# Gate and up of a SwiGLU layer as a 2x2 block product, one pair of k-tiles in eight by Strassen's seven products

## The chip, the core and the metric

The kernel runs on one core of a Trainium2 chip. It uses TensorE (matrix products into PSUM, eight banks of 128 x 512 floats), VectorE and ScalarE (elementwise work, casts, evictions from PSUM), SyncE as the queue that issues the loads of weights, and ScalarE's queue for a few other transfers. The metric is device time in microseconds, the median of the runs shown; lower is better.

## The reference, cut to what matters

A decoder block over 256 tokens with a width of 2048: normalised input, projections, attention and mLSTM heads, an output projection with a residual, then the SwiGLU layer that is changed here, a gated embedding at the end. All inputs are float32.

```
h2 = rms_norm(x, w_norm_ffn[i])
x = x + (jax.nn.silu(h2 @ w_ffn_gate[i]) * (h2 @ w_ffn_up[i])) @ w_ffn_down[i]
```

h2 is 256 x 2048, w_ffn_gate and w_ffn_up are 2048 x 5632, w_ffn_down is 5632 x 2048.

## The kernel before, in words

Every large product goes through `linear` (line 210). The contraction is cut into k-tiles of 128 rows; the output into chunks of 512 columns; the 256 tokens into two blocks of 128 (b = 0, 1), each with its own PSUM accumulator, acc0 and acc1. A product in float32 is made of three matmuls on a reduced type: activations and weights are each split into a high half (a cast to float32r) and a low half (what the cast left off), and high x high, high x low of the weights, and low of the activations x high are added up in PSUM (lines 255, 256, 257). The activations are the stationary operand, 512 columns of weights stream past.

Weights come in pieces of two k-tiles, 128 x 1024 floats: a load on SyncE's queue into `wr` (line 229), ScalarE's cast to `wh` (line 230), VectorE's subtraction to `wl` (line 231). The pool `wpool` has four buffers of each. A piece serves 12 matmuls.

Gate and up take 11 chunks (`for c in range(NG)`, line 643). For a chunk, all 16 k-tiles of the gate weights go through `linear`, then ScalarE's sigmoid (line 649) and a multiply-add by VectorE (line 650) evict the two accumulators to `gg`; then the same for the up weights with one multiply-add each (line 653). The product is then split for the next layer by background tasks (`after_up`, `split_by_blocks`, `transposed`): VectorE transposes it in blocks of 32 (line 187, tile `tq`), ScalarE's queue writes it to DRAM in four transfers (`swap`, line 191) and reads it back in another layout (`quad`, line 196), and ScalarE and VectorE make high and low halves (lines 129, 130). `tq` and `quad` have one buffer each; `held` keeps two tasks from using them at once. The activations of the layer itself come in four quarters through the same path from the residual (lines 628, 133, 135).

The code is written as a stream; a scheduler then sets the order on each engine by its own estimate of times, and every engine runs its queue strictly in that order. After the last chunk the input p is loaded into a `gg0` buffer (line 660), transposed on TensorE (line 165) and split, and w_down's product follows.

## Time and profile before

| | us |
|---|---|
| median of three runs (1228.24 to 1229.06) | 1228.42 |
| the profiled execution | 1229.32 |
| span of its instructions | 1227.6 |
| TensorE busy | 1215.7 |
| VectorE busy | 706.0 |
| ScalarE busy | 585.9 |

A page of the profile gives busy time by engine; `PE` is TensorE's matmul, `PEld` its weight load, `DVE` VectorE, `ACT` ScalarE, `SPq` and `ACTq` the queues that issue transfers. `L231` is line 231 of the kernel. A matmul's printed duration is longer than the distance to the next one, since matmuls overlap.

### The profile page before, as it was taken

How to read it: one execution, taken by the hardware profiler on the slowest of the kernel's cores; microseconds unless marked ns; L12 is line 12 of the kernel's file. 1: busy time of each engine (PE TensorE's matmuls, PEld its weight loads, DVE VectorE, ACT ScalarE, POOL GpSimd, SP SyncE). 2: the span in 40 equal slices, each digit the busy share in tenths (PEclk: the TensorE clock that was granted, in tenths of full speed). 3: DMA queues.
4: the chain of work that ended last, by engine and by line, in shares of the span. 5: the costliest groups of instructions: out<-in, count | busy, mean ns of one | idle time of the engine just before them, and what ended most of it. 6: DMA issues, size and time to landing. Idle time of an engine off the chain costs nothing.

```text
span 1227.6 us, 15262 instructions
## 1 busy us (share of the span) xinstructions
PE 1215.7 (99%) x5675; PEld 1017.9 (83%) x5675; DVE 706.0 (58%) x948; ACT 585.9 (48%) x822; POOL 4.5 (0%) x24
## 2 busy tenths in 40 slices
PE   9999999999999999999999999999999999999998
PEld 6799978878888888888888888888888888888888
DVE  5566755555656655555665564655545555555754
ACT  6645555645545534443443443444444444446542
POOL 1000000000000000000000000000000000000000
PEclk9999999999999999999999999999999999999999
DMA  7578754675677776766776677677666666665672
GB/s 262 175 238 246 219 153 124 186 240 160 208 229 251 238 222 200 231 207 213 227 226 205 217 231 211 205 229 223 208 218 200 220 198 220 204 212 169 220 248 88
DMA packets 158781, 257.30 MB, mean 210 GB/s; under 512 B 10002, under 2 KB 54900, under 8 KB 158708
## 3 DMA queue, kind: packets, MB, share of 16 engines
q1 hardware_dynamic: 127156, 229.06, 59.6%
q10 hardware_dynamic: 31552, 27.28, 7.4%
q8 instruction: 44, 0.72, 0.2%
q14 instruction: 29, 0.24, 0.1%
HBM read 241.10 MB, written 15.20 MB: 209 GB/s over the span
## 4 chain that ended last, share of the span: by engine, by line
PE 88%; DMA 4%; DVE 3%; ACT 2%; issue 1%; ACTq 0%; SPq 0%; DVEq 0%
PE acc L256 29%; PE acc L257 28%; PE acc L255 28%; DMA wr<-in_w_in_dram 3%; DVE wl L231 1%; DMA wpost<-in_w_ple_post_norm_dram 1%; ACT wh L230 1%; ACT sq L116 1%; DMA quad<-swap 0%; DMA swap<-tq 0%; DVE m L376 0%; PE sc L551 0%; ACT act_h L690 0%; PE tr L165 0%; PE tr L568 0%
## 5 line engine op out<-in xcount | busy, mean ns | idle before, releaser
L231 DVE TENSOR_TENSOR wl<-wr,wh 128x1024 fp32r<-128x1024 f32 (+2 forms) x445 | 520.1, 1181 | 399.6 <-ACT wh L230 398.7
L230 ACT CAST wh<-wr 128x1024 fp32r<-128x1024 f32 (+2 forms) x445 | 447.2, 1018 | 519.4 <-PE acc L257 383.0
L255 PE MATMUL acc<-wh,act_h 128*128 128x512 f32 (+2 forms) x1568 | 593.1, 379 | 3.2 <-ACT wh L230 1.9
L256 PE MATMUL acc<-wl,act_h 128*128 128x512 f32 (+2 forms) x1568 | 591.4, 377 | 1.6 <-DVE wl L231 1.5
L257 PE MATMUL acc<-wh,act_l 128*128 128x512 f32 (+2 forms) x1568 | 591.2, 377 | 0.0
L255 PEld LDWEIGHTS acc<-wh,act_h 128*128 128x128 f32 x1568 | 294.6, 188 | 55.3 <-ACT wh L230 2.2
L256 PEld LDWEIGHTS acc<-wl,act_h 128*128 128x128 f32 x1568 | 294.8, 188 | 53.5 <-DVE wl L231 3.4
L257 PEld LDWEIGHTS acc<-wh,act_l 128*128 128x128 f32 x1568 | 294.7, 188 | 51.9 <-DVE act_l L135 0.6
L255 PE MATMUL acc<-wh,gh 128*128 128x512 f32 x224 | 88.0, 393 | 0.0
L256 PE MATMUL acc<-wl,gh 128*128 128x512 f32 x224 | 87.9, 393 | 0.0
L257 PE MATMUL acc<-wh,gl 128*128 128x512 f32 x224 | 87.1, 389 | 0.0
L257 PEld LDWEIGHTS acc<-wh,gl 128*128 128x128 f32 x224 | 42.0, 188 | 9.5
L255 PEld LDWEIGHTS acc<-wh,gh 128*128 128x128 f32 x224 | 42.1, 188 | 9.4
L256 PEld LDWEIGHTS acc<-wl,gh 128*128 128x128 f32 x224 | 42.1, 188 | 8.6
L133 ACT ACTIVATE act_h<-quad,vec_b 128x256 fp32r<-128x256 f32 x32 | 13.7, 498 | 22.5 <-DMA quad<-swap 22.5
L135 DVE SCALAR_TENSOR_TENSOR act_l<-quad,vec_b,act_h 128x256 fp32r<-128x256 f32 x32 | 13.5, 483 | 16.1 <-ACT act_h L133 16.1
L649 ACT ACTIVATE gg<-acc,rstd_ffn 128x512 f32<-128x512 f32 x22 | 15.1, 689 | 10.8 <-PE acc L257 10.8
L650 DVE SCALAR_TENSOR_TENSOR gg<-acc,rstd_ffn,gg 128x512 f32<-128x512 f32 x22 | 15.8, 751 | 4.7 <-ACT gg L649 4.5
L130 DVE TENSOR_TENSOR gl<-quad,gh 128x512 fp32r<-128x512 f32 x14 | 9.1, 688 | 16.2 <-ACT gh L129 16.2
L129 ACT CAST gh<-quad 128x512 fp32r<-128x512 f32 x14 | 8.0, 618 | 20.6 <-DMA quad<-swap 20.6
L653 DVE SCALAR_TENSOR_TENSOR gg<-acc,rstd_ffn,gg 128x512 f32<-128x512 f32 x22 | 15.4, 743 | 0.0
L116 ACT ACTIVATE sq<-xres 128x512 bf16<-128x512 f32 x24 | 14.9, 623 | 0.0
(192 smaller groups left out, 392.1 us busy)
## 6 DMA issues: line engine op xcount, KB each, us to landing
wr<-in_w_ffn_gate_dram SPq DMA_DIRECT2D x88, 512.0 KB, 4.3
wr<-in_w_ffn_up_dram SPq DMA_DIRECT2D x88, 512.0 KB, 4.7
wr<-in_w_ffn_down_dram SPq DMA_DIRECT2D x88, 512.0 KB, 4.6
wr<-in_w_in_dram SPq DMA_DIRECT2D x63, 512.0 KB, 4.8
wr<-in_w_in_dram SPq DMA_DIRECT2D x48, 344.0 KB, 3.8
wr<-in_w_out_dram SPq DMA_DIRECT2D x32, 512.0 KB, 4.7
wr<-in_w_ple_gate_dram SPq DMA_DIRECT2D x32, 512.0 KB, 4.7
swap<-tq ACTq DMA_DIRECT2D x100, 128.0 KB, 4.4
```

The lines of the kernel that those rows point to most:

```text
L116: nc.scalar.activation(sq[:, 0:n], src, AF.Square, accum_out=dst)
L130: nc.vector.tensor_tensor(lo, src, hi.bitcast(F32), op=ALU.subtract)
L133: nc.scalar.activation(part(dst[0], k + j, 1), src[:, j:j + 1], AF.Copy, scale=scales[j])
L135: nc.vector.scalar_tensor_tensor(part(dst[1], k + j, 1), src[:, j:j + 1], scales[j], part(dst[0], k + j, 1).bitcast(F32), op0=ALU.mult, op ...
L230: nc.scalar.copy(wh, wr)
L231: nc.vector.tensor_tensor(wl, wr, wh.bitcast(F32), op=ALU.subtract)
L255: nc.tensor.matmul(po[b][:, 0:n], ah[:, kk, s], wh[:, j, :], start=count == 1, stop=False)
L256: nc.tensor.matmul(po[b][:, 0:n], ah[:, kk, s], wl[:, j, :], start=False, stop=False)
L257: nc.tensor.matmul(po[b][:, 0:n], al[:, kk, s], wh[:, j, :], start=False, stop=count == total)
L649: nc.scalar.activation(gg[b], pg[b], AF.Sigmoid, scale=r)
L650: nc.vector.scalar_tensor_tensor(gg[b], pg[b], r, gg[b], op0=ALU.mult, op1=ALU.mult)
L653: nc.vector.scalar_tensor_tensor(gg[b], pu[b], rstd2[:, b:b + 1], gg[b], op0=ALU.mult, op1=ALU.mult)
```

## The change

The gate and the up weights of a chunk are taken together. A pair of k-tiles p (rows of A: two k-tiles of the activations, each with two token blocks; rows of B: the same two k-tiles of gate and of up) is a 2x2 by 2x2 block product with four outputs: gate and up for b = 0 and b = 1. Seven of the eight pairs are "plain" units: eight products, 24 matmuls, accumulated in four banks P2, P3, P4, P8 (tags acc0, acc1, acc0, acc1). Pair 1 is a "seven" unit: seven products P1 to P7, 21 matmuls, of sums of the blocks. P2, P3 and P4 go into the plain units' banks; P1, P5, P6, P7 have banks of their own (tags tr and sc, which are the banks of transposes and scores elsewhere), so all eight banks hold accumulators.

The sums of activation blocks are made once (`make_forms`, in the first chunk); the sums of weight blocks (`t12`, `t34`) by VectorE for every chunk, and they are split into halves like weights. So a plain unit has two casts and two subtractions of 1024 columns; the seven unit has three and a half of each, four buffers. In the first chunk the seven unit stands fourth, in the others first. P1, P6, P7 and P5 are evicted into `qr` (tile quad) and `su` (tile tq) some units later, P2, P4, P3, P8 at the end of the chunk. `gg` has one buffer for each b now; `p_sb` shares it; `wpost` gets the two buffers of `sg`.

```diff
+    def halves(wr):
+
+        k, n = wr.shape[1:]
+        wh, wl = (wpool.tile([P, 1024], F32R, name=name)[:, 0:k * n].rearrange("p (k n) -> p k n", k=k)
+                  for name in ("wh", "wl"))
+        nc.scalar.copy(wh, wr)
+        nc.vector.tensor_tensor(wl, wr, wh.bitcast(F32), op=ALU.subtract)
+        return wh, wl
...
+        seven = (1,)
+        first_order, later_order = (0, 2, 3, 1, 4, 5, 6, 7), (1, 0, 2, 3, 4, 5, 6, 7)
...
+        def make_forms(p):
+
+            while held:
...
+            fa = quads.tile([P, 2, 2, P], F32, name="tq")
...
+            f = quads.tile([P, 4, P], F32, name="quad")
+            a11, a12, a21, a22 = fa[:, 0, 0], fa[:, 1, 0], fa[:, 0, 1], fa[:, 1, 1]
+            nc.vector.scalar_tensor_tensor(f[:, 0], a21, -1.0, a22, op0=ALU.mult, op1=ALU.subtract)
+            nc.vector.scalar_tensor_tensor(f[:, 1], f[:, 0], -1.0, a11, op0=ALU.mult, op1=ALU.subtract)
+            nc.vector.tensor_tensor(f[:, 2], a11, a21, op=ALU.subtract)
+            nc.vector.tensor_tensor(f[:, 3], a12, f[:, 1], op=ALU.subtract)
...
+            nc.scalar.copy(fh, f)
+            nc.vector.tensor_tensor(fl, f, fh.bitcast(F32), op=ALU.subtract)
+            forms[p] = {"P1": (h[:, k, 0:P], l[:, k, 0:P]), "P2": (h[:, k + 1, 0:P], l[:, k + 1, 0:P]),
+                        "P4": (h[:, k + 1, P:2 * P], l[:, k + 1, P:2 * P]),
+                        **{n: (fh[:, i], fl[:, i]) for i, n in enumerate(("P5", "P6", "P7", "P3"))}}
...
+        def plain_unit(c, p, acts):
+
+            w2 = [halves(load_piece(w, 2 * p, 2, c * 512, 512)) for w in (w_gate, w_up)]
+            out = []
+            for j in range(2):
+                h, l = acts
+                k = 2 * (p % 2) + j
+                for b in range(2):
+                    t = slice(b * P, (b + 1) * P)
+                    for i in range(2):
+                        out.append((("P2", "P3", "P4", "P8")[2 * b + i], (h[:, k, t], l[:, k, t]),
+                                    (w2[i][0][:, j, :], w2[i][1][:, j, :])))
+            return out
+
+        def seven_unit(c, p):
+            ra, rb = (load_piece(w, 2 * p, 2, c * 512, 512) for w in (w_gate, w_up))
+            t12 = fp.tile([P, 2, 512], F32, name="wt", bufs=2)
+            nc.vector.tensor_tensor(t12[:, 0], ra[:, 0], rb[:, 0], op=ALU.subtract)
+            nc.vector.tensor_tensor(t12[:, 1], t12[:, 0], rb[:, 1], op=ALU.add)
+            t34 = fp.tile([P, 2, 512], F32, name="wt", bufs=2)
+            nc.vector.tensor_tensor(t34[:, 0], t12[:, 1], ra[:, 0], op=ALU.subtract)
+            nc.vector.tensor_tensor(t34[:, 1], ra[:, 1], t12[:, 1], op=ALU.subtract)
+            ah, al = halves(ra)
+            h12, l12 = halves(t12)
+            bh, bl = halves(rb[:, 1:2])
+            h34, l34 = halves(t34)
+            right = {"P1": (ah[:, 0], al[:, 0]), "P6": (h12[:, 1], l12[:, 1]), "P5": (h12[:, 0], l12[:, 0]),
+                     "P2": (ah[:, 1], al[:, 1]), "P7": (h34[:, 0], l34[:, 0]), "P4": (h34[:, 1], l34[:, 1]),
+                     "P3": (bh[:, 0], bl[:, 0])}
+            return [(n, forms[p][n], v) for n, v in right.items()]
+
+        def gate_up(c):
+            tags = {"P1": "tr", "P6": "tr", "P7": "sc", "P5": "sc", "P2": "acc0", "P3": "acc1", "P4": "acc0", "P8": "acc1"}
+            order = first_order if c == 0 else later_order
+            left = {"P1": len(seven), "P6": len(seven), "P7": len(seven), "P5": len(seven), "P8": 16 - 2 * len(seven),
+                    **{n: 16 - len(seven) for n in ("P2", "P3", "P4")}}
+            bank, t1, qr, su = {}, None, None, None
+            for p in order:
+                advance(1)
+                if p in seven:
+                    while p not in forms:
+                        advance(1)
+                    unit = seven_unit(c, p)
+                else:
+                    h = acts_h[p // 2]
+                    unit = plain_unit(c, p, h)
+                    while id(h[0]) in made_by and not made_by[id(h[0])].done:
+                        advance(2)
+                advance(1)
+                for n, (lh, ll), (rh, rl) in unit:
+                    first = n not in bank
+                    if first:
+                        bank[n] = ps.tile([P, 512], F32, name=tags[n])
+                    left[n] -= 1
+                    nc.tensor.matmul(bank[n], lh, rh, start=first, stop=False)
+                    nc.tensor.matmul(bank[n], lh, rl, start=False, stop=False)
+                    nc.tensor.matmul(bank[n], ll, rh, start=False, stop=left[n] == 0)
+                if su is None and left["P1"] == 0:
+                    while held:
+                        advance(1)
+                    t1 = fp.tile([P, 512], F32, name="sg", bufs=2)
+                    nc.scalar.copy(t1, bank["P1"])
+                    qr = quads.tile([P, 2, 512], F32, name="quad")
+                    nc.vector.tensor_tensor(qr[:, 0], bank["P6"], t1, op=ALU.add)
+                    nc.vector.tensor_tensor(qr[:, 1], bank["P7"], qr[:, 0], op=ALU.add)
+                    su = quads.tile([P, 2, 512], F32, name="tq")
+                    for i in range(2):
+                        nc.vector.tensor_tensor(su[:, i], bank["P5"], qr[:, i], op=ALU.add)
+            gg = [fp.tile([P, 512], F32, name=f"gg{b}") for b in range(2)]
+            nc.vector.tensor_tensor(gg[0], bank["P2"], t1, op=ALU.add)
+            nc.vector.tensor_tensor(gg[1], bank["P4"], qr[:, 1], op=ALU.add)
+            nc.vector.tensor_tensor(su[:, 0], bank["P3"], su[:, 0], op=ALU.add)
+            nc.vector.tensor_tensor(su[:, 1], bank["P8"], su[:, 1], op=ALU.add)
+            for b in range(2):
+                r = rstd2[:, b:b + 1]
+                sg = fp.tile([P, 512], F32, name="sg", bufs=2)
+                nc.scalar.activation(sg, gg[b], AF.Sigmoid, scale=r)
+                nc.vector.scalar_tensor_tensor(gg[b], gg[b], r, sg, op0=ALU.mult, op1=ALU.mult)
+                nc.vector.scalar_tensor_tensor(gg[b], su[:, b], r, gg[b], op0=ALU.mult, op1=ALU.mult)
+            return gg
...
         for c in range(NG):
-            pg = linear(w_gate, acts_h, c * 512, 512, width=1)
-            gg = [None, None]
-            for b in range(2):
-                gg[b] = fp.tile([P, 512], F32, name=f"gg{b}", bufs=2)
-                r = rstd2[:, b:b + 1]
-                nc.scalar.activation(gg[b], pg[b], AF.Sigmoid, scale=r)
-                nc.vector.scalar_tensor_tensor(gg[b], pg[b], r, gg[b], op0=ALU.mult, op1=ALU.mult)
-            pu = linear(w_up, acts_h, c * 512, 512, width=1)
-            for b in range(2):
-                nc.vector.scalar_tensor_tensor(gg[b], pu[b], rstd2[:, b:b + 1], gg[b], op0=ALU.mult, op1=ALU.mult)
+            if c == 0:
+                for kp in seven:
+                    Task(make_forms(kp), [made_by[id(acts_h[kp // 2][0])]])
+            gg = gate_up(c)
...
-        p_sb = fp.tile([P, 512], F32, name="gg0", bufs=2).rearrange("p (b k) -> p b k", b=2)
+        p_sb = fp.tile([P, 512], F32, name="gg0").rearrange("p (b k) -> p b k", b=2)
         nc.sync.dma_start(out=p_sb, in_=p.rearrange("(b p) k -> p b k", p=P))
-        acts_p = (fp.tile([P, 2, 256], F32R, name="ph"), fp.tile([P, 2, 256], F32R, name="pl"))
+        acts_p = [fp.tile([P, 4, 256], F32R, name="wt", bufs=2)[:, 0:2] for _ in range(2)]
...
-                wpost = fp.tile([P, 512], F32, name="wpost")
+                wpost = fp.tile([P, 512], F32, name="sg", bufs=2)
-                g = fp.tile([P, 512], F32, name=f"gg{b}", bufs=2)[:, 0:n]
+                g = fp.tile([P, 512], F32, name=f"gg{b}")[:, 0:n]```

VectorE's queue at the end of a chunk, **before**: the two evictions of up (L653), the transposes, then weight work. `gg0` and `gg1` are the two token blocks of the gated product.

```order
L231 TENSOR_TENSOR wl_5739<-wr_5737,wh_5738 128x1024
L653 SCALAR_TENSOR_TENSOR gg0_5535<-acc0_5541,rstd_ffn_3072,gg0_5535 128x512
L653 SCALAR_TENSOR_TENSOR gg1_5538<-acc1_5542,rstd_ffn_3072,gg1_5538 128x512
L187 STREAM_TRANSPOSE tq_5693<-gg0_5535 128x512
L187 STREAM_TRANSPOSE tq_5693<-gg1_5538 128x512
L231 TENSOR_TENSOR wl_5759<-wr_5757,wh_5758 128x1024
```

**Now**, at the same place, from P4's eviction (L754, behind those of P2 and P3) on. `wl_4863` and `wl_4867` are the low halves bl and l34 of the seven unit, `wl_4920` that of the first plain unit's gate weights.

```order
L754 TENSOR_TENSOR gg1_4826<-acc0_4550,quad_4566 128x512
L761 SCALAR_TENSOR_TENSOR gg0_4825<-gg0_4825,rstd_ffn_3072,sg_4831 128x512
L756 TENSOR_TENSOR tq_4569<-acc1_4593,tq_4569 128x512
L762 SCALAR_TENSOR_TENSOR gg0_4825<-tq_4569,rstd_ffn_3072,gg0_4825 128x512
L761 SCALAR_TENSOR_TENSOR gg1_4826<-gg1_4826,rstd_ffn_3072,sg_4835 128x512
L221 TENSOR_TENSOR wl_4863<-wr_4846,wh_4862 128x512
L762 SCALAR_TENSOR_TENSOR gg1_4826<-tq_4569,rstd_ffn_3072,gg1_4826 128x512
L221 TENSOR_TENSOR wl_4867<-wt_4851,wh_4866 128x1024
L187 STREAM_TRANSPOSE tq_4841<-gg0_4825 128x512
L187 STREAM_TRANSPOSE tq_4841<-gg1_4826 128x512
L221 TENSOR_TENSOR wl_4920<-wr_4917,wh_4919 128x1024
```

Nine instructions of evictions and transposes stand around the two subtractions of the seven unit and ahead of the next unit's; all ten boundaries between chunks have these rows.

TensorE's queue in the same chunk, **now**, from the fifteenth matmul behind the boundary to the twenty-sixth; the fourteen ahead of them are P1, P6, P5 and P2 with three matmuls each and the first of P7 and of P4.

```order
L738 MATMUL acc1_4899<-wh_4862,fh1_3898 128x512
L738 MATMUL acc0_4887<-wh_4919,act_h_3249 128x512
L739 MATMUL acc1_4899<-wl_4863,fh1_3898 128x512
L740 MATMUL acc1_4899<-wh_4862,fl1_3899 128x512
L738 MATMUL acc1_4899<-wh_4925,act_h_3249 128x512
L738 MATMUL acc1_4938<-wh_4925,act_h_3249 128x512
L739 MATMUL sc_4891<-wl_4867,fh1_3898 128x512
L740 MATMUL sc_4891<-wh_4866,fl1_3899 128x512
L739 MATMUL acc0_4895<-wl_4867,act_h_3249 128x512
L740 MATMUL acc0_4895<-wh_4866,act_l_3250 128x512
L738 MATMUL acc0_4895<-wh_4919,act_h_3249 128x512
L739 MATMUL acc0_4887<-wl_4920,act_h_3249 128x512
```

The scheduler has mixed the seven unit (`wh_4862`, `wl_4867`) with the first plain unit (`wh_4919`, `wh_4925`); the last row is the first that reads `wl_4920`.

SyncE's queue at the end of the last chunk, **before**: p's load stands between loads of up weights, into a `gg0` buffer that is free.

```order
L229 DMA wr_7195<-in_w_ffn_up_dram 128x2x512
L229 DMA wr_7213<-in_w_ffn_up_dram 128x2x512
L660 DMA gg0_7271<-in_p_dram 128x2x256
L229 DMA wr_7231<-in_w_ffn_up_dram 128x2x512
L229 DMA wr_7249<-in_w_ffn_up_dram 128x2x512
```

**Now** it is behind six pieces of w_down and both loads of wpost; these are the last of them.

```order
L212 DMA wr_7718<-in_w_ffn_down_dram 128x2x512
L795 DMA sg_9540<-in_w_ple_post_norm_dram 128x512
L795 DMA sg_9580<-in_w_ple_post_norm_dram 128x512
L212 DMA wr_7738<-in_w_ffn_down_dram 128x2x512
L212 DMA wr_7756<-in_w_ffn_down_dram 128x2x512
L776 DMA gg0_7601<-in_p_dram 128x2x256
L212 DMA wr_7774<-in_w_ffn_down_dram 128x2x512
```

The load moved from before the end of the up weights to behind w_down's eighth piece, and it waits for the transpose that reads the `gg0` of the last chunk.

## Rows read from the trace of the kernel before

**Rows 1.** The page, part 1: busy us (share of the span), instructions.

```profile
PE 1215.7 (99%) x5675; PEld 1017.9 (83%) x5675; DVE 706.0 (58%) x948; ACT 585.9 (48%) x822; POOL 4.5 (0%) x24
```

**Rows 2.** Busy time by stretch, gate and up: PE, PEld, DVE, ACT, POOL, clock, DMA, GB/s.

```profile
401.30:879.90 478.60, 478.60 (x2113) 396.32 (x2112) 272.22 (x280) 210.22 (x226) 0.00 (x0) 1.00 0.71 219
```

**Rows 3.** Waits of the whole program: us in total, times, longest us.

```profile
DVE wl L231 <- ACT wh L230: 398.7, 301, 5.3
ACT wh L230 <- PE acc L257: 383.0, 252, 4.8
...
PEld acc L256 <- DVE wl L231: 3.4, 6, 0.9
```

**Rows 4.** Timeline, gate chunk, TensorE and ScalarE: start us, us, instruction, [idle before].

```profile
646.53 0.39 PE L257 MATMUL acc<-wh,act_l 128*128 128x512 f32 x1
...
646.96 1.05 ACT L230 CAST wh<-wr 128x1024 fp32r<-128x1024 f32 x1 [1.67 <-PE acc L257]
```

**Rows 5.** Groups by shape: busy us, mean ns | idle us before.

```profile
L231 DVE TENSOR_TENSOR wl<-wr,wh 128x1024 fp32r<-128x1024 f32 x395 | 478.0, 1221 | 377.5 <-ACT wh L230 376.9
L230 ACT CAST wh<-wr 128x1024 fp32r<-128x1024 f32 x395 | 410.2, 1051 | 482.8 <-PE acc L257 362.8 <-issue 49.0 <-DMA swap<-tq 39.8
...
L650 DVE SCALAR_TENSOR_TENSOR gg<-acc,rstd_ffn,gg 128x512 f32<-128x512 f32 x22 | 15.8, 751 | 4.7 <-ACT gg L649 4.5
...
L562 DVE TENSOR_SCALAR prob<-prob,rsum 128x128 f32<-128x128 f32 x8 | 2.3, 287 | 0.3
L231 DVE TENSOR_TENSOR wl<-wr,wh 128x512 fp32r<-128x512 f32 x2 | 1.4, 692 | 1.9 <-ACT wh L230 1.9
L230 ACT CAST wh<-wr 128x512 fp32r<-128x512 f32 x2 | 1.2, 620 | 3.3 <-DMA wr<-in_w_in_dram 3.3
```

**Rows 6.** Timeline of VectorE where its instructions stand back to back.

```profile
400.53 1.23 DVE L231 TENSOR_TENSOR wl<-wr,wh 128x1024 fp32r<-128x1024 f32 x1 [0.90 <-ACT wh L230]
401.67 1.28 DVE L628 TENSOR_TENSOR xres<-acc,xres 128x512 f32<-128x512 f32 x2
402.87 1.29 DVE L187 STREAM_TRANSPOSE tq<-xres 128x512 f32<-128x512 f32 x2
404.09 1.18 DVE L231 TENSOR_TENSOR wl<-wr,wh 128x1024 fp32r<-128x1024 f32 x1
...
662.79 1.41 DVE L653 SCALAR_TENSOR_TENSOR gg<-acc,rstd_ffn,gg 128x512 f32<-128x512 f32 x2
664.11 1.29 DVE L187 STREAM_TRANSPOSE tq<-gg 128x512 f32<-128x512 f32 x2
```

**Rows 7.** TensorE behind a wait, and a stretch with waits (columns as in rows 2).

```profile
60.59 0.42 PE L256 MATMUL acc<-wl,act_h 128*128 128x344 f32 x1 [0.60 <-DVE wl L231]
60.85 0.32 PE L257 MATMUL acc<-wh,act_l 128*128 128x344 f32 x1
...
0.00:10.00 10.00, 7.69 (x30) 4.16 (x30) 2.70 (x6) 3.62 (x6) 4.49 (x24) 1.00 0.77 242
```

**Rows 8.** The round trip of a gated chunk: ScalarE's timeline, and issues (us to landing).

```profile
665.44 2.58 ACTq L191 DMA_DIRECT2D swap<-tq  x4
...
swap<-tq ACTq DMA_DIRECT2D x100, 128.0 KB, 4.4
quad<-swap ACTq DMA_DIRECT2D x25, 512.0 KB, 5.7
```

**Rows 9.** ScalarE and VectorE, the residual's last quarter.

```profile
417.22 1.71 ACT L133 ACTIVATE act_h<-quad,vec_b 128x256 fp32r<-128x256 f32 x4 [2.98 <-DMA quad<-swap]
...
417.76 1.69 DVE L135 SCALAR_TENSOR_TENSOR act_l<-quad,vec_b,act_h 128x256 fp32r<-128x256 f32 x4 [2.09 <-ACT act_h L133]
```

**Rows 10.** p's load and transposes, and loads of its size: KB, us to landing.

```profile
856.44 0.46 SPq L660 DMA_DIRECT2D gg<-in_p_dram  x1
...
880.69 0.60 PE L165 MATMUL tr<-ident,gg 128*128 128x128 f32 x4
...
wpost<-in_w_ple_post_norm_dram SPq DMA_DIRECT2D x4, 256.0 KB, 4.4
```

More of the change, by code (lines that the diff above doesn't have):

```diff
@@ L208, in split_by_blocks, with load_piece @@
         held.pop()
+    def load_piece(w, kt, nk, c0, n):
+        wr = wpool.tile([P, 1024], F32, name="wr")[:, 0:nk * n].rearrange("p (k n) -> p k n", k=nk)
+        nc.sync.dma_start(out=wr, in_=w[kt * P:(kt + nk) * P, c0:c0 + n].rearrange("(k p) n -> p k n", p=P))
+        return wr
+    def halves(wr):
[5 more added lines that the diff above has]
+        return wh, wl
     def linear(w, acts, c0, n, pieces=None, before=None, load=None, width=2):
@@ L223, in fetch @@
                 load(kt)
-            def piece(name, dt):
-                return wpool.tile([P, 1024], dt, name=name)[:, 0:nk * n].rearrange("p (k n) -> p k n", k=nk)
-            wr, wh, wl = piece("wr", F32), piece("wh", F32R), piece("wl", F32R)
-            nc.sync.dma_start(out=wr, in_=w[kt * P:(kt + nk) * P, c0:c0 + n].rearrange("(k p) n -> p k n", p=P))
-            nc.scalar.copy(wh, wr)
-            nc.vector.tensor_tensor(wl, wr, wh.bitcast(F32), op=ALU.subtract)
-            ready.append((wh, wl))
+            ready.append(halves(load_piece(w, kt, nk, c0, n)))
         for i, (kt, nk) in enumerate(pieces):
@@ new lines, in block_kernel @@
+        first_order, later_order = (0, 2, 3, 1, 4, 5, 6, 7), (1, 0, 2, 3, 4, 5, 6, 7)
+        forms = {}
+        def make_forms(p):
+            while held:
+                yield held
+            held.append(p)
+            h, l = acts_h[p // 2]
+            k = 2 * (p % 2)
+            fa = quads.tile([P, 2, 2, P], F32, name="tq")
+            fh = fp.tile([P, 4, P], F32R, name=f"fh{p}")
+            fl = fp.tile([P, 4, P], F32R, name=f"fl{p}")
+            nc.vector.tensor_tensor(fa.rearrange("p k b t -> p k (b t)"), h[:, k:k + 2, :].bitcast(F32),
+                                    l[:, k:k + 2, :].bitcast(F32), op=ALU.add)
+            yield
+            f = quads.tile([P, 4, P], F32, name="quad")
[4 more added lines that the diff above has]
+            nc.vector.tensor_tensor(f[:, 3], a12, f[:, 1], op=ALU.subtract)
+            yield
+            nc.scalar.copy(fh, f)
[3 more added lines that the diff above has]
+                        **{n: (fh[:, i], fl[:, i]) for i, n in enumerate(("P5", "P6", "P7", "P3"))}}
+            held.pop()
+            yield
@@ L702, in block_kernel @@
             for b in range(2):
-                g = fp.tile([P, 512], F32, name=f"gg{b}", bufs=2)[:, 0:n]
+                g = fp.tile([P, 512], F32, name=f"gg{b}")[:, 0:n]
                 nc.scalar.activation(g, po[b], AF.Sigmoid, scale=rstd3[:, b:b + 1])
```

## The prediction

> **What bounds the kernel now.** I read the busy shares of the page first, then the stage of gate and up, then who waits for whom. TensorE is busy 99% of the span, VectorE 58%, ScalarE 48% [rows 1]. In the stage that is changed, 478.6 us long, TensorE is busy through all of it at a granted clock of 1.00 (its 2.4 GHz level), VectorE 272.22 us and ScalarE 210.22 us [rows 2]. The waits say the same from the other side: ScalarE's casts wait for TensorE to give a weight buffer back (383.0 us), VectorE's subtractions wait for the casts (398.7 us), and what TensorE waits for sums to a few us in the whole program [rows 3]. So the matmuls set the time, and each costs its distance from issue to issue, not the 0.39 us that a row prints [rows 4]: 478.60 us for the stage's 2112 (11 chunks of 192) are 0.2267 us each [rows 2].
>
> **What is taken away.** A pair of k-tiles costs 2 k-tiles x 2 token blocks x 2 weights x 3 = 24 matmuls; seven products cost 21. One pair in eight, eleven chunks: 33 matmuls fewer of 5675, all of 512 columns, and that is all the gain there is: 33 x 0.2267 = **7.5 us**. TensorE is the bound, so all of it counts if nothing else makes TensorE wait.
>
> **What is added, on average.** Per chunk VectorE gets four weight sums of 512 columns (0.69 us each, as the subtraction of that size), 1.5 more subtractions of 1024 (1.22), and twelve evictions and sums instead of four, eight more at 0.69 or less [rows 5]: 2.8 + 1.8 + 5.5 = 10 us on top of 272.22 / 11 = 24.7, in 42.8 us. ScalarE gets 1.5 casts (1.05) and a copy, 2.2 us on 19.1. By averages all fits, VectorE at 81%. Weight bytes stay. But the work is not spread: it falls together where a chunk ends and the next begins.
>
> **The chunk's boundary.** Let T be the moment at which the last unit of a chunk is issued and the seven products of the next could start. I walk VectorE's queue in the order of the change section. The last unit ends P2, P3, P4 and P8 in this order, three matmuls apart, so P4's last matmul is issued 4 x 0.227 before T. A reader starts 0.43 us after the issue of the last matmul (646.53 to 646.96) [rows 4], so the eviction of P4 starts at T - 0.48. VectorE is free for it: the two evictions ahead of it (P2, P3) are paced by TensorE in the same steps of 0.68. From there VectorE waits for nobody and goes through ten more instructions. Back to back they stand closer than they last: a subtraction of 1024 from 400.53 to 401.67, so 1.14; two 512-column additions from there to 402.87, so 0.60 each; two transposes to 404.09, so 0.61; two multiply-adds from 662.79 to 664.11, so 0.66 [rows 6]. The queue: P4's eviction 0.60, multiply-add 0.66, P8's eviction 0.60 (its matmuls ended at T + 0.20, earlier), three multiply-adds 1.98 with the subtraction for bl of 0.61 between them, the subtraction for l34 1.14, two transposes 1.22, and only then the low half of the next unit's gate weights, 1.22 to its end: 8.03 us, with 0.1 for one result read at once by the next instruction, so it is there at T + 7.65. ScalarE isn't later: two sigmoids of 512 columns (0.62 as the cast of that size, or a little more) and casts of 0.62 or 1.05 [rows 5] stand in its queue with gaps.
>
> TensorE has 25 matmuls ahead of the one that wants this half (the matmul rows of the change section end there), 25 x 0.2267 = 5.67 us. It waits 7.65 + 0.04 - 5.67 = 2.0 us, and a matmul behind a wait lasts 0.1 us longer than the next (0.42 and 0.32, at 60.59) [rows 7]. So 2.1 us; earlier waits in these 25 (for casts and for l34) are inside it, and the up half, 1.14 later, comes with 6 matmuls between and is in time. At the other end, if each instruction took its whole duration (0.69, 0.75, 1.22) plus 0.04, the chain from T - 0.48 is 9.3 us and the wait 3.2. I take **2.2 us**, near the rows that stand back to back, since this queue is of just such rows. There are ten such boundaries with the same queue: **22 us**, from 16 (1.6 each, if some starts early) to 32.
>
> The Trainium skill's "VectorE: DVE Perf Modes", section "The DRAIN you can't avoid", says that the next VectorE operation does not start until the pipe of the one before is empty, though one that nothing holds starts earlier. By the first half of that rule the ten waits would come to the upper end, 32 us; the rows, 1.14 apart at 1.23 long, side with the second half, and the measurement decides.
>
> Does the delay go on? The next three units (16 us) need 2 x 1.22 of VectorE each in 5.44, so it catches up. The round trip of the gated chunk through DRAM now stands ahead of weight work in both queues: swaps issued at T + 6.4 to 9.1 (2.58 us for four), landed 4.4 us later, read back in another 5.7 (medians) [rows 8], near T + 19; behind it two casts, two subtractions and the cast and subtraction for the up weights of the unit that starts at T + 23.2 (93 matmuls and the wait): ready near T + 22.5, asked for four matmuls into the unit, at T + 24.1. Margin 1.6 us: **0** on the middle, with up to 1 us a chunk on the high side.
>
> **The first chunk** has the seven products as fourth unit, at S + 16.3, where S = 401.3 is the stage's start. Its activation forms need the buffer "quad", which until then holds the last quarter of the residual's activations: read by ScalarE from 417.22 to 418.93 and by VectorE to 419.45 [rows 9]. Then VectorE: 0.61, three sums of 128 columns (0.29 each), 1.14, another sum: 422.4; ScalarE's cast of the forms 0.62: 423.1; and their low halves after one 1024 subtraction, 424.2. TensorE could do 16 matmuls before it needs these, from 417.6 to 421.2. So **3 us**, 2 to 4, once.
>
> **The last chunk.** The load of p took a free buffer at 856.44, 24 us before its use at 880.69. Now it goes into the only gg0, so behind the transpose of gg0 (T + 6.4) and, on SP's queue, behind two wpost and two weight loads, the later of which waits for a subtraction ending near T + 5.8. A load of this size lands after 4.4 us (wpost) [rows 10], behind the others perhaps a us later: T + 11.3 to 12.5. TensorE has 44 matmuls ahead of p's transposes, 10 us, and all later matmuls of w_down queue behind them: **2 us**, 0 to 3. wpost with two buffers saves nothing: TensorE is covered there.
>
> **The sum.** -7.5 + 22 + 3 + 2 = +19.5 us. The profiled execution took 1229.32 us, span 1227.6 and 1.7 around it; with the sum 1248.8. It is 0.9 us above the median of 1228.42, so the median becomes **1248 us**, 1.6% slower. Ends of the terms: -7.5 + 16 + 2 + 0 = +10.5 and -7.5 + 32 + 4 + 3 = +31.5, so 1239 to 1260.
>
> **Rivals.**
> *Not slower: VectorE clears the boundary in time.* If the chain from P4's eviction to the gate's low half fits in 5.67 + 0.48 = 6.15 us instead of 8.1, the ten waits vanish: 1228.4 - 7.5 + 5 = 1226 us, or 1221 with the single waits gone too. For it: the average of 81%, and evictions that are started by TensorE early. Against it: that point lies 24% below rows that already stand back to back. 6 in 100.
> *The delay runs through the chunk.* If the swap and its read back take 2 to 3 us more than their medians, the unit at T + 23 waits too, 1 to 2 us in each of ten chunks: 1258 to 1268 us. For it: ScalarE's casts already wait 39.8 us for swaps in all [rows 5]. Against it: the 1.6 us of margin. 9 in 100.
> *The clock falls.* If each wait at a boundary dropped TensorE to its 1.2 GHz level for one unit of 24 matmuls, that would be 24 x 0.227 = 5.4 us more, ten times: 1302 us. Against it: in the first 10 us TensorE is busy for 7.69, and the granted clock is 1.00 [rows 7]. 2 in 100. The Trainium skill's "TensorE: Matmul & The Clock Gate", section "A second HAM failure mode: psum-queue depth-cycling", tells of a kernel whose short pauses between groups in changing PSUM banks made the clock swing; nothing here shows that.
> *It doesn't do what it says.* If the products were not saved, the time would be 1256. TensorE's queue has 33 rows fewer, so 1 in 100.
>
> **How the numbers follow.** Forecast 82 in 100. Faster or slower by under 0.2% is about what a measurement of this kernel can tell from no change, so 1226.0 to 1230.9 counts as the same. The first rival gives faster 0.05 and the edge of same; with a forecast whose waits are all much smaller, same gets 0.03; slower 0.92. The range 1239 to 1260 leaves out the first rival, the clock and half of the second, with a rest of the forecast.
>
> **What would show it.** Right: ten gaps of about 2 us on TensorE, all at the matmul that waits for VectorE's low half of the first plain unit's gate weights, just after two transposes; VectorE without idle time from P4's eviction to there; one gap near 420 us for the forms, one at p's transposes. Wrong: matmuls 0.227 apart across a boundary (the chain is shorter than I say), or waits for DMA in the middle of a chunk (the second rival), or a granted clock under 1.00.

## The result, and the profile after

The change makes the kernel slower: **1248.89 us** (median of 4 runs, 1246.40 to 1249.23) against 1228.33 us, a ratio of 1.0159 with a 95% interval of [1.0147, 1.0171]. The profiled execution has a span of 1247.0 us, 19.4 more than the 1227.6 of before. The page's part 1, the answer to [rows 1], is:

```profile
PE 1221.0 (98%) x5642; PEld 1009.8 (81%) x5642; DVE 806.2 (65%) x1108; ACT 606.5 (49%) x856; POOL 4.5 (0%) x24
```

TensorE has its 33 matmuls fewer, and VectorE 100 us more, 9.1 per chunk. Where [rows 3] had a few us of TensorE's waits, the same view of after (us in total, times, longest us) has a new first line:

```profile
PE acc L739 <- DVE wl L221: 10.8, 11, 1.9
...
PE tr L165 <- DMA gg<-in_p_dram: 1.9, 1, 1.9
PE sc L739 <- DVE wl L221: 1.5, 9, 0.2
```

Eleven waits for the low half of a weight piece, ten of them at the chunks' boundaries and one, the longest, in the first chunk. Here is a boundary on VectorE, then TensorE in the same moments (start us, us, instruction, idle before it); T, the issue of the first seven-product matmul, is 581.74:

```profile
579.90 0.69 DVE L753 TENSOR_TENSOR gg<-acc,sg 128x512 f32<-128x512 f32 x1 [0.63 <-PE acc L740]
580.58 0.69 DVE L755 TENSOR_TENSOR tq<-acc,tq 128x512 f32<-128x512 f32 x1
581.26 0.69 DVE L754 TENSOR_TENSOR gg<-acc,quad 128x512 f32<-128x512 f32 x1
581.87 0.74 DVE L761 SCALAR_TENSOR_TENSOR gg<-gg,rstd_ffn,sg 128x512 f32<-128x512 f32 x1
...
585.72 1.22 DVE L221 TENSOR_TENSOR wl<-wt,wh 128x1024 fp32r<-128x1024 f32 x1
586.85 1.30 DVE L187 STREAM_TRANSPOSE tq<-gg 128x512 f32<-128x512 f32 x2
588.07 3.46 DVE L221 TENSOR_TENSOR wl<-wr,wh 128x1024 fp32r<-128x1024 f32 x3
```

```profile
581.74 0.39 PE L738 MATMUL tr<-wh,act_h 128*128 128x512 f32 x1
...
587.00 0.50 PE L739 MATMUL sc<-wl,fh 128*128 128x512 f32 x1 [0.17 <-DVE wl L221]
...
589.32 0.50 PE L739 MATMUL acc<-wl,act_h 128*128 128x512 f32 x1 [0.89 <-DVE wl L221]
```

P4's eviction (L754) starts at T - 0.48; behind it no row of VectorE has idle time; the two transposes stand just ahead of the low half; and the matmul that reads it is issued at T + 7.58 and not at T + 5.67. The printed 0.89 us is only a part of that delay: the scheduled order puts other waiting matmuls ahead of it (0.17 us at 587.00, and some near 586 that are issued over 0.3 us apart without a printed wait). The whole delay is read from the chunk's period: the first matmul of P1 is issued at 447.09 in the second chunk and at 851.43 nine chunks later, 44.93 us per chunk, where 189 matmuls at 0.2267 are 42.85. So each boundary costs **2.1 us**.

The whole stage, from its first matmul to the first one behind it (before, that is a transpose of p; now w_down's, since p's transposes stand 44 matmuls later), took 495.6 us (400.7 to 896.3), before 478.7 (402.0 to 880.7): +16.9. What lies behind it, with p's wait, took 350.7 us and before 346.9: +3.8. What lies ahead took 1.3 less; this part is not changed, and the stage begins anywhere from 400.7 to 402.2 us in the runs below.

### The profile page after: what moved, and what is told of

Read it like the earlier page. It is cut to its first block, busy times and chain, and to the rows that moved or that the text cites. A ratio compares the mean times of both kernels' runs of the same rounds, so it can differ in the third digit from the quotient of the medians.

```text
span 1247.0 us, 15443 instructions
## 1 busy us (share of the span) xinstructions
PE 1221.0 (98%) x5642; PEld 1009.8 (81%) x5642; DVE 806.2 (65%) x1108; ACT 606.5 (49%) x856; POOL 4.5 (0%) x24
## 4 chain that ended last, share of the span: by engine, by line
PE 86%; DVE 9%; DMA 3%; issue 1%; ACT 1%; SPq 0%; DVEq 0%; ACTq 0%
PE acc L263 17%; PE acc L264 17%; PE acc L262 17%; PE acc L739 11%; PE acc L740 10%; PE acc L738 10%; DVE wl L221 2%; DMA wr<-in_w_in_dram 2%; DVE tq L187 1%; DVE gg L761 1%; DVE gg L762 1%; DVE gg L753 1%; DVE tq L755 1%; DVE gg L754 1%; DVE tq L756 1%
## 5 line engine op out<-in xcount | busy, mean ns | idle before, releaser
L221 DVE TENSOR_TENSOR wl<-wr,wh 128x1024 fp32r<-128x1024 f32 (+2 forms) x445 | 511.8, 1167 | 324.0 <-ACT wh L220 322.9
L220 ACT CAST wh<-wr 128x1024 fp32r<-128x1024 f32 (+2 forms) x445 | 440.5, 1007 | 507.0 <-PE acc L264 220.8
L262 PE MATMUL acc<-wh,act_h 128*128 128x512 f32 (+2 forms) x864 | 319.2, 371 | 3.0 <-ACT wh L220 1.9
L263 PE MATMUL acc<-wl,act_h 128*128 128x512 f32 (+2 forms) x864 | 317.4, 367 | 1.5 <-DVE wl L221 1.5
L264 PE MATMUL acc<-wh,act_l 128*128 128x512 f32 (+2 forms) x864 | 317.3, 367 | 0.0
L739 PE MATMUL acc<-wl,act_h 128*128 128x512 f32 x638 | 247.9, 391 | 10.8 <-DVE wl L221 10.8
L740 PE MATMUL acc<-wh,act_l 128*128 128x512 f32 x638 | 246.7, 389 | 0.0
L738 PE MATMUL acc<-wh,act_h 128*128 128x512 f32 x638 | 245.4, 393 | 1.0 <-ACT wh L220 0.9
L262 PEld LDWEIGHTS acc<-wh,act_h 128*128 128x128 f32 x864 | 162.5, 188 | 28.0 <-ACT wh L220 2.5
L263 PEld LDWEIGHTS acc<-wl,act_h 128*128 128x128 f32 x864 | 162.7, 188 | 25.5 <-DVE wl L221 2.7
L264 PEld LDWEIGHTS acc<-wh,act_l 128*128 128x128 f32 x864 | 162.5, 188 | 24.2 <-DVE act_l L135 0.6
L739 PEld LDWEIGHTS acc<-wl,act_h 128*128 128x128 f32 x638 | 119.8, 188 | 40.4 <-DVE wl L221 15.8
L738 PEld LDWEIGHTS acc<-wh,act_h 128*128 128x128 f32 x638 | 119.0, 188 | 32.1 <-ACT wh L220 8.3
L740 PEld LDWEIGHTS acc<-wh,act_l 128*128 128x128 f32 x638 | 119.8, 188 | 24.7
L263 PE MATMUL acc<-wl,gh 128*128 128x512 f32 x224 | 88.9, 397 | 0.0
L264 PE MATMUL acc<-wh,gl 128*128 128x512 f32 x224 | 88.0, 393 | 0.0
L264 PEld LDWEIGHTS acc<-wh,gl 128*128 128x128 f32 x224 | 42.5, 190 | 9.6
L263 PEld LDWEIGHTS acc<-wl,gh 128*128 128x128 f32 x224 | 42.4, 189 | 8.7
L760 ACT ACTIVATE sg<-gg,rstd_ffn 128x512 f32<-128x512 f32 x22 | 15.9, 721 | 30.8 <-DVE gg L753 30.8
L221 DVE TENSOR_TENSOR wl<-wt,wh 128x1024 fp32r<-128x1024 f32 x22 | 26.8, 1219 | 0.0
## 6 DMA issues: line engine op xcount, KB each, us to landing
wr<-in_w_ffn_gate_dram SPq DMA_DIRECT2D x88, 512.0 KB, 4.5
wr<-in_w_ffn_up_dram SPq DMA_DIRECT2D x88, 512.0 KB, 4.6
wr<-in_w_ffn_down_dram SPq DMA_DIRECT2D x88, 512.0 KB, 4.6
wr<-in_w_in_dram SPq DMA_DIRECT2D x63, 512.0 KB, 4.7
wr<-in_w_out_dram SPq DMA_DIRECT2D x32, 512.0 KB, 4.9
wr<-in_w_ple_gate_dram SPq DMA_DIRECT2D x32, 512.0 KB, 4.7
swap<-tq ACTq DMA_DIRECT2D x100, 128.0 KB, 4.6
```

What stands on the lines that cost most here:

```text
L220: nc.scalar.copy(wh, wr)
L221: nc.vector.tensor_tensor(wl, wr, wh.bitcast(F32), op=ALU.subtract)
L262: nc.tensor.matmul(po[b][:, 0:n], ah[:, kk, s], wh[:, j, :], start=count == 1, stop=False)
L263: nc.tensor.matmul(po[b][:, 0:n], ah[:, kk, s], wl[:, j, :], start=False, stop=False)
L264: nc.tensor.matmul(po[b][:, 0:n], al[:, kk, s], wh[:, j, :], start=False, stop=count == total)
L738: nc.tensor.matmul(bank[n], lh, rh, start=first, stop=False)
```

## Experiments

All are compared with the kernel before on the same chip: medians 1228.75 us (e1 to e4), 1228.14 (e5 to e8) and 1228.53 (e9 and e10). The change itself ran against 1228.33, so a difference to it goes across chips whose medians of the kernel before lie up to 0.6 us apart.

**e1: the chain at the boundary made shorter.** The transposes of the finished chunk go behind the low halves of the first plain unit.

```diff
         def after_up(dst, gg):
+            for _ in range(3):
+                yield
...
-                if su is None and left["P1"] == 0:
+                if su is None and left["P1"] == 0 and (c == 0 or p != 1):
```

> The two transposes of the gated chunk are given out three steps later, so that on VectorE they stand behind the low halves of the next plain unit's gate and up weights instead of ahead of them; the first eviction of the seven products moves back by one unit with them. Nothing is left out. Theory (VectorE's queue at the chunk's boundary makes TensorE wait): the gate's low half comes two transposes, 1.2 us, earlier, the wait of 2.1 us at each of ten boundaries falls to about 0.9, and the time by 12 us, to 1236 to 1238 us. Rival (the casts that wait for TensorE to give weight buffers back set the pace, and VectorE's order does not matter): no change, 1249 us.

Measured: **1233.81 us** (1233.51 to 1234.94), ratio 1.0042 [1.0027, 1.0057]; 15 us of the change's 20 are gone. The period is 43.72 us (577.31 less 533.59 for the first matmul of P1), so 0.9 us are left at a boundary. Two transposes that stand 0.61 us from their neighbours left VectorE's queue ahead of the half that TensorE wants, and each boundary became 1.2 us shorter, 12 us in all. The other 3 are not the boundaries': the first chunk's longest wait is 0.99 us in this trace and not 1.88, and the clock stays up behind p's wait (last section).

**e6: the chain made longer by one instruction.** This is the opposite dose; the same sum is written twice.

```diff
-            nc.vector.tensor_tensor(gg[1], bank["P4"], qr[:, 1], op=ALU.add)
+            for _ in range(2):
+                nc.vector.tensor_tensor(gg[1], bank["P4"], qr[:, 1], op=ALU.add)
```

> The change with one eviction add at each chunk's end written twice (the same sum into the same tile), one more 512-column VectorE instruction in the chain ahead of the low halves, and nothing else in the order of the engines moved. Back to back such instructions stand 0.61 to 0.69 us apart. My theory (TensorE waits at each of ten boundaries for the end of this chain): +6 to +7 us, 1255 to 1256 us. Rival (the wait is set by something else, a cast on ScalarE or a load, and VectorE is only the last name on it): within 1 us of 1249 us.

Measured: **1253.84 us** (1253.49 to 1256.31), ratio 1.0210 [1.0193, 1.0227]: +5.0 us, a little under the 6 to 7 expected, far from the rival's 0. The period is 45.47 us (584.10 less 538.63), and 45.69 on the mean of nine, two of which are longer than the rest: one instruction that stands 0.60 us from its neighbour lengthens a boundary by some 0.55. The chain sets the wait, instruction by instruction.

**e4: the bank-per-product code without the products.** No unit uses seven products; the other accumulators stay, evicted by four instructions. All 192 matmuls per chunk are there.

```diff
-        seven = (1,)
+        seven = ()
...
-                if su is None and left["P1"] == 0:
+                if False:
...
-            nc.vector.tensor_tensor(gg[0], bank["P2"], t1, op=ALU.add)
-            nc.vector.tensor_tensor(gg[1], bank["P4"], qr[:, 1], op=ALU.add)
-            nc.vector.tensor_tensor(su[:, 0], bank["P3"], su[:, 0], op=ALU.add)
-            nc.vector.tensor_tensor(su[:, 1], bank["P8"], su[:, 1], op=ALU.add)
...
```

> All eight pairs are plain units of 24 matmuls; no sums of blocks and no seven products; gate and up are evicted from their four banks as in the kernel before. Nothing else is left out, and 33 matmuls more are done than in the changed kernel. Theory (the extra VectorE work makes the waits, not the block form): the boundaries fit again; the time is that of the kernel before plus the 3.5 us at p, and up to 0.3 us a boundary for banks that come free late: 1230 to 1235 us. Rival (taking gate and up together halves how far the weights are made ahead, and that makes the waits): 1249 us or more.

Measured: **1230.55 us** (10 runs, 1229.67 to 1231.19), ratio 1.0014 [1.0004, 1.0024]. TensorE waits for no low half in the stage, which takes 480.3 us, 1.6 more than before. Running gate and up as one stream with four accumulators costs little; the waits come with VectorE's work for the seven products. This run takes the sums, the extra halves and the evictions out together, so it does not say which of them counts.

**e3: the seven products in the middle of the chunk.** If only the boundary were tight, this would free it.

```diff
-            order = first_order if c == 0 else later_order
+            order = first_order
```

> The unit of seven products stands fourth in every chunk, as it does in the first, so away from the evictions at the chunk's end. Nothing is left out. Simple reading (two piles of VectorE work that meet at the boundary): apart, both fit, the ten waits go, and what is left is the first chunk's 3 us and the 3.5 us at p: 1228.4 - 7.5 + 6.5 = 1227 us. My theory (what counts is what stands ahead of the next plain unit's low halves in VectorE's queue): behind the seven unit there now stand the two subtractions of the gated chunk, which wait for its read back near 19.6 us after the boundary, and the evictions of P1, P6, P7 and P5; the next unit's low halves come 2 to 3.5 us late, in each of ten chunks: 1245 to 1258 us, about as slow as the changed kernel.

Measured: **1254.32 us** (1253.37 to 1257.81), ratio 1.0212 [1.0196, 1.0228], slower still. TensorE's waits in the stage and, at one of them, ScalarE (as above):

```profile
PE acc L738 <- ACT wh L220: 14.9, 21, 1.7
PE acc L739 <- DVE wl L221: 2.0, 1, 2.0
```

```profile
601.22 0.58 ACT L745 COPY sg<-tr 128x512 f32<-128x512 f32 x1
603.98 1.14 ACT L129 CAST act_h<-quad 128x512 fp32r<-128x512 f32 x2 [2.19 <-DMA quad<-swap]
605.02 3.88 ACT L220 CAST wh<-wr 128x1024 fp32r<-128x1024 f32 x4
```

TensorE now waits for ScalarE, whose casts for the next unit stand behind two casts that wait 2.19 us for the round trip through DRAM. The boundary is clear, and the delay has a new place. In this order the prediction's second rival, the round trip standing ahead of weight work, is what happens. My range held, but I had looked for the delay in VectorE's queue, and it stands in ScalarE's. Part of the time is of another kind: in this trace the clock fell four times in mid chunk (last section), for some 3 us each, by my estimate 1.5 us of time each. If the other executions had them too, e3 would without them be about as slow as the change.

**e5: the first chunk.** One number moves: the seven products come fifth there.

```diff
-        first_order, later_order = (0, 2, 3, 1, 4, 5, 6, 7), (1, 0, 2, 3, 4, 5, 6, 7)
+        first_order, later_order = (0, 2, 3, 4, 1, 5, 6, 7), (1, 0, 2, 3, 4, 5, 6, 7)
```

> The change with one number moved: in the first chunk the seven-product unit comes fifth and not fourth, so that its four differences stand on VectorE behind the low halves of the unit before it. The trace after shows two waits in the first chunk, 1.88 and 0.93 us, about 3.0 us in all against 189 matmuls at 0.2267 us. My theory (the differences stand ahead of the low halves and wait for the up half's load): most of the 3 us goes, 1246 to 1247 us. Rival (the first chunk is late by its loads, whatever stands first on VectorE): 1248.5 to 1249.5 us.

Measured: **1245.95 us** (1244.72 to 1246.87), ratio 1.0146 [1.0131, 1.0161]: -2.9 us. From its first matmul to that of the next chunk the first chunk takes 43.1 us in this trace (402.22 to 445.36); in after it is 46.4 (400.70 to 447.09). So 3.3 us go there. The boundary behind it, though, is 1.2 us longer than the others (46.15 us from P1 to the next chunk's P1): VectorE's first difference of the second chunk waits 2.52 us for its up weights there, and the evictions behind it begin after the chunk's end (445.41) and not 1.8 us before it.

**e2: p's load.** p has a tile of its own, loaded at the last chunk's start.

```diff
+        p_sb = fp.tile([P, 512], F32, name="p_sb").rearrange("p (b k) -> p b k", b=2)
         for c in range(NG):
+            if c == NG - 1:
+                nc.sync.dma_start(out=p_sb, in_=p.rearrange("(b p) k -> p b k", p=P))
...
-        p_sb = fp.tile([P, 512], F32, name="gg0").rearrange("p (b k) -> p b k", b=2)
-        nc.sync.dma_start(out=p_sb, in_=p.rearrange("(b p) k -> p b k", p=P))
```

> p gets a buffer of its own and its load is issued long before the last chunk ends. Nothing is left out. Theory: the one gap of 1.9 us at p's transposes goes, and with it the stretch of slower matmuls behind it (granted clock 0.51 from 910 to 912 us), some 1.5 us more: 3.5 us less than the changed kernel, 1245.4 us. Rival (the slow stretch has nothing to do with the gap): 1.9 us less, 1247 us, and the clock falls at the same place. Second rival (another wait stands behind it): no change.

Measured: **1246.35 us** (1243.96 to 1246.88), ratio 1.0138 [1.0123, 1.0153]: -2.5 us. No wait is left at p's transposes, and the clock does not fall there in this trace. By the time, which lies between my 3.5 us and the rival's 1.9 with runs that spread over 2.9, the two are not told apart.

**e7: all waits out of the way, the products kept.** Besides e5's edit, a free tile for p, e1's later first eviction and P3 drawn ahead of P7 and P4, three things, in their core: the SwiGLU products go behind the low halves (into `after_up`), the half unit has its own tiles, and in each unit the matmuls that need no low half of a weight come first (in the seven unit from its sixth product on).

```diff
-        def after_up(dst, gg):
+        def after_up(dst, gg, su):
+            held.append(su)
+            for _ in range(3):
+                yield
...
-            bh, bl = halves(rb[:, 1:2])
+            bh, bl = (fp.tile([P, 1, 512], F32R, name=name) for name in ("bh", "bl"))
...
+                work = [(n, a, b) for n, (lh, ll), (rh, rl) in unit for a, b in ((lh, rh), (lh, rl), (ll, rh))]
+                k = 15 if p in seven else 0
+                work = work[:k] + [w for i, w in enumerate(work[k:]) if i % 3 != 1] + work[k + 1::3]
...
```

> The change with VectorE's load at a chunk's end taken out of TensorE's way: the SwiGLU products follow behind the low halves of the first plain unit, the half unit of the up weights has its own tiles, each unit's matmuls that need no low half come first, the seven-product unit is fifth in the first chunk, and p's tile is one that is free earlier. The number of matmuls is that of the change, 33 under the kernel before. My theory (the sum without its three waits is -7.5 us, and up to 2 us of them may stay): 1221 to 1224 us. Rival (VectorE's added work of about 9 us per chunk comes back as waits at another place, or the shorter product form is worth less than its matmuls): 1228 us or more.

Measured: **1222.45 us** (1221.94 to 1223.51), ratio 0.9956 [0.9941, 0.9971], span 1220.3: faster than both kernels. A boundary on VectorE (T is 530.56), and the stretch from the second chunk to 6 us behind the stage (columns as in [rows 2]):

```profile
530.76 0.68 DVE L768 TENSOR_TENSOR gg<-acc,sg 128x512 f32<-128x512 f32 x1
531.36 0.68 DVE L769 TENSOR_TENSOR gg<-acc,quad 128x512 f32<-128x512 f32 x1
531.96 0.68 DVE L770 TENSOR_TENSOR tq<-acc,tq 128x512 f32<-128x512 f32 x1
532.55 0.68 DVE L771 TENSOR_TENSOR tq<-acc,tq 128x512 f32<-128x512 f32 x1
533.15 1.21 DVE L221 TENSOR_TENSOR wl<-wt,wh 128x1024 fp32r<-128x1024 f32 x1
534.29 2.35 DVE L221 TENSOR_TENSOR wl<-wr,wh 128x1024 fp32r<-128x1024 f32 x2
536.56 1.41 DVE L655 SCALAR_TENSOR_TENSOR gg<-gg,rstd_ffn,sg 128x512 f32<-128x512 f32 x2
```

```profile
446.00:880.00 434.00, 434.00 (x1915) 358.75 (x1914) 332.15 (x384) 210.82 (x233) 0.00 (x0) 1.00 0.68 220
```

Only the four evictions stand ahead of the low halves, which TensorE moreover wants later. It is busy for all of the 434 us, 0.2266 us per matmul as before, while VectorE is busy 77% of them. VectorE's work is that of the change to within one per cent (800.8 us against 806.2); what differs is the order, on VectorE and on TensorE. So the amount was not what cost time. These edits were made together; apart from e1, e5 and e2, which tried parts of them, no run says what each is worth.

**e8, e9, e10: two pairs of eight by seven products.** These have 33 (e8) or 30 matmuls fewer again, and no room for the half unit's own tiles. e8 places the second unit sixth; e9 and e10 have one such unit in the first chunk, and in the later ones this order:

```diff
-        seven = (1,)
-        first_order, later_order = (0, 2, 3, 1, 4, 5, 6, 7), (1, 0, 2, 3, 4, 5, 6, 7)
+        seven = (1, 5)
+        first_order, later_order = (0, 2, 3, 4, 1, 5, 6, 7), (0, 1, 2, 3, 4, 6, 5, 7)
```

e10 has (0, 2, 1, 3, 4, 6, 5, 7) as the last of these.

> As e7_relief, with two of eight pairs of k-tiles by seven products (the second sixth in the later chunks), 33 matmuls fewer again, but without own tiles for the half unit, for which there is no room. My theory: -7.5 us more if the second unit's casts come in time, 1214 to 1218 us; the run with the seven-product unit in fourth place showed ScalarE's casts late by some 1.4 us per chunk, and with that it would be 1226 to 1232 us. I hold the second for somewhat less likely. Rival (the block form saves nothing by itself): as e7_relief or slower.

> As e8_two_pairs, but each later chunk begins with a plain unit, the two seven-product units stand second and seventh, and the first chunk has one seven-product unit only. A plain unit's casts need no buffer that the last unit of the chunk before still holds, so VectorE's low halves for it can be made ahead of the evictions. If the 2 us per boundary of e8 came from the tiles that its first unit waits for, and its 3.4 us in the first chunk from the second unit there: 1214 to 1220 us (e7 less 30 matmuls at 0.2267 us, 6.8 us, plus what waits are left). Rival (two seven-product units give VectorE and ScalarE more than they can do in a chunk of 42.2 us, wherever they stand): 1232 us or more, as e8.

> As e9_two_apart with the first of the two seven-product units third and not second, two plain units behind the chunk's end. VectorE has 5.4 us more for it, but its first transpose of the finished chunk now stands among the unit's differences. First theory: within 2 us of e9, on either side. Rival as for e9: 1232 us or more.

Measured: **1237.28** (1235.85 to 1238.15), **1233.38** (1232.36 to 1236.68) and **1229.55 us** (10 runs, 1226.44 to 1235.78); ratios 1.0075 [1.0060, 1.0090], 1.0044 [1.0028, 1.0060] and 1.0011 [0.9997, 1.0024]. None keeps e7's gain. e8 missed both of my figures; its rival's figure fits, but not its reason, since TensorE's waits make the loss. e9 came out as its rival said, and e10 lies 4 us under e9, further than I gave it, and under that rival's 1232 us: the place of a unit counts. In e8 the period is 44.2 us (580.69 to 624.92), where 186 matmuls are 42.2; in e10 639 matmuls stand in a stretch that holds 662 in e7. In e10, TensorE's waits and a stretch of the stage:

```profile
PE tr L754 <- DVE wl L221: 4.1, 9, 0.6
PE acc L754 <- DVE gg L767: 2.0, 10, 0.2
```

```profile
600.00:750.00 150.00, 147.48 (x639) 118.97 (x638) 128.30 (x154) 76.72 (x88) 0.00 (x0) 1.00 0.68 215
```

VectorE is the engine most waited for, busy 128.30 of 150 us, 86%. But the printed waits of e10's stage, 6.4 us, are under half of what is lost: its period is 43.6 us (455.38 to 847.90 for nine chunks) where 186 matmuls are 42.2. What the rest is was not followed up. Whether a better order would fit two pairs in, or there is no such order, these runs leave open.

## Why the prediction was right

The forecast was 1248 us from -7.5 + 22 + 3 + 2, and the mechanism it names, VectorE's queue at ten boundaries, is the one that e1, e4 and e6 show. That the total came within 1 us is in part luck: the boundaries came 1.2 us lower, what lies ahead of the stage 1.3 lower, the part behind it 1.8 higher and the first chunk 0.5 higher.

- **The gain, -7.5 us: right as a price, and most of it is seen.** e7, almost without waits, lies 5.7 us under the kernel before by the medians (1222.45 to 1228.14), and its stage is 6.4 us shorter (472.4 us, from 401.46 to 873.83, against 478.7). Its chunks take 42.91 us (444.75 to 830.91 for nine), 0.06 over their 189 matmuls, and the first chunk 0.4 over; that is most of what is missing to 7.5. The stage before was read some 0.7 us too early, as 401.30 to 879.90: its 2112 matmuls begin at 401.96 and what follows them at 880.69, which leaves 0.2267 us for each.
- **The boundaries, 22 us: right in place, cause and size.** Ten delays of 2.1 us for 2.2 predicted, at the named matmul, issued at T + 7.58 where T + 7.69 had been worked out. The taken value, from rows that stand back to back, was the right end: rows of 0.69 us start 0.60 to 0.68 apart in after too. This is also what the trace makes of the Trainium skill's "VectorE: DVE Perf Modes", section "The DRAIN you can't avoid": its second half, the earlier start of an operation that nothing holds, fits these rows. e1 and e6 then made the chain two instructions shorter and one longer, and the period followed by 1.2 and some 0.55 us. e4 shows that the waits go with VectorE's new work.
- **The first chunk, 3 us: right in size, with one of two paths overlooked.** The first chunk took 46.4 us (above), 3.5 over its 42.85. But TensorE does not wait for the forms in the trace. Its two waits there are these:

```profile
413.85 0.50 PE L739 MATMUL acc<-wl,act_h 128*128 128x512 f32 x1 [1.88 <-DVE wl L221]
...
421.95 0.50 PE L738 MATMUL acc<-wh,act_h 128*128 128x512 f32 x1 [0.93 <-ACT wh L220]
```

and VectorE ahead of the first:

```profile
409.91 0.69 DVE L701 TENSOR_TENSOR wt<-wr 128x512 f32<-128x512 f32 x1 [3.46 <-DMA wr<-in_w_ffn_up_dram]
...
412.58 2.35 DVE L221 TENSOR_TENSOR wl<-wr,wh 128x1024 fp32r<-128x1024 f32 x2
```

  The four differences of the seven products' weights stand ahead of two low halves of the unit before, and the first of them waits 3.46 us for the up weights. I had walked ahead from the forms and had not asked what the differences themselves wait for and who stands behind them. The second wait is for a cast on ScalarE. The forms came about when they were worked out to come, their low halves at 423.77 (for 424.2):

```profile
423.09 0.68 DVE L677 TENSOR_TENSOR fl<-quad,fh 128x512 fp32r<-128x512 f32 x1
```

  The first matmul that reads these low halves has 88 ahead of it in the chunk, so without the two waits it would have been due at 420.65 (88 times 0.2267 behind 400.70) and would have waited for them: an estimated 3 us, or 2 with the forms as early as in e5 (22.1 us behind the chunk's first matmul and not 23.1). So two paths of about the same length end here, the earlier waits cover the forms', and the size came out though I had only one of them. e5 puts the unit 24 matmuls later, which clears both, and leaves 0.3 us; it does not tell them apart.
- **p's load, 2 us: the wait right, at 1.86 us; what came behind it was not foreseen.** The clock fell there (last section), and the part behind the stage grew by 3.8 us in the profiled execution. In e1, e3 and e5, with waits of 1.80, 2.00 and 1.53 us and no fall, it grew by 1.6, 1.8 and 1.3. I had weighed the clock at the boundaries alone. By medians e2 gives 2.5 us back.
- **The rivals.** VectorE did not clear in time; e7 shows an order in which it does: five instructions from the first eviction to the half, where the change has twelve. The delay did not run on through the chunk: period and boundary agree. In e3, where the seven products stand fourth, the round trip does decide. The clock stayed at 1.00 through every boundary.

## What to carry to other kernels

A change that takes work off the engine that bounds the time should be costed at the moments where the work it adds to other engines falls together, not by their averages: VectorE at 77% cost next to nothing in e7, and at nearly the same work 2.1 us at every boundary in the change. At such a place, walk the queue of the other engine row by row from the last thing it waits for to the thing that is waited for, and count from the rows' distance, not their length. Then put first in that queue what the bounding engine needs next, and let the bounding engine begin with what is ready. e7 does both; alone, only the first was tried (e1).

## What was not expected of the hardware

A wait of TensorE of one to two us can be followed by its lower clock level, and most are not. Behind p's transposes in after, the matmuls are 0.43 us apart instead of 0.23, and the granted clock is near one half (1.2 GHz) for some 3 us, then 1.00 again:

```profile
908.40 1.02 PE L165 MATMUL tr<-ident,gg 128*128 128x128 f32 x4 [1.86 <-DMA gg<-in_p_dram]
...
910.07 0.63 PE L263 MATMUL acc<-wl,gh 128*128 128x512 f32 x1
910.50 0.63 PE L264 MATMUL acc<-wh,gl 128*128 128x512 f32 x1
...
908.00:910.00 2.00, 1.60 (x6) 1.48 (x7) 0.00 (x0) 0.54 (x1) 0.00 (x0) 0.64 1.03 370
910.00:912.00 2.00, 2.00 (x6) 1.53 (x5) 1.53 (x2) 1.88 (x3) 0.00 (x0) 0.51 0.56 172
912.00:914.00 2.00, 2.00 (x10) 1.61 (x10) 1.52 (x2) 0.26 (x1) 0.00 (x0) 1.00 0.25 50
```

In e6 the same place had a wait of 2.41 us and the same fall; in e1 (1.80 us), e3 (2.00) and e5 (1.53) there was none, nor behind the 1.88 us at 413.85 in after. e3 had four in mid chunk, behind waits of 1.50, 1.28, 1.60 and 1.70 us, and none behind its waits of 1.52 us at 515.08 and 1.28 at 744.73.

The clearest case stands near 60 us, far ahead of the changed stage, where TensorE has the same two waits in every run, of 1.90 and 0.5 to 0.6 us. There the clock falls in e4, e5, e6, e7, e9 and e10, and stays up in before, after, e1, e2, e3 and e8. One and the same stretch of after, then of e7:

```profile
62.00:64.00 2.00, 2.00 (x14) 2.00 (x13) 1.96 (x4) 0.51 (x1) 0.00 (x0) 1.00 0.83 290
62.00:64.00 2.00, 2.00 (x9) 2.00 (x8) 1.97 (x4) 0.49 (x1) 0.00 (x0) 0.50 0.86 300
```

So neither the length of the wait nor the instructions around it settle whether the clock falls; what does is left open here. A difference of a us or two between two kernels can be a fall of this kind, and the granted clock by stretch tells.
